# Seven half-size products for most tile pairs of both feed-forward stages, with the second matrix in five chunks

## Chip, cores and metric

The kernel runs on one core of a Trainium2 chip. The metric is the device time of one execution in microseconds (us); lower is better. All arithmetic is on fp32 data; the large products run on TensorE in its fp32r format, in three passes (below).

## What is computed

A trunk layer on h = 16 learned tokens followed by 512 tokens, 1024 features:

```python
h = h + 0.5 * rmsnorm(swiglu(rmsnorm(h, n[0]), ffn1_wi, ffn1_wo), n[1])
h = h + rmsnorm(hybrid_mixer(rmsnorm(h, n[2]), ...), n[3])
h = h + 0.5 * rmsnorm(swiglu(rmsnorm(h, n[4]), ffn2_wi, ffn2_wo), n[5])

def swiglu(x, wi, wo):                    # wi: 1024 x 5632, wo: 2816 x 1024
    a, b = jnp.split(x @ wi, 2, axis=-1)
    return (jax.nn.silu(a) * b) @ wo
```

The change touches the two feed-forward stages (`swiglu`). The mixer between them (Fourier, short convolution, gated DeltaNet) stays as it is.

## The kernel before

Features lie on the 128 partitions, tokens along the free dimension: `hT` is [128, 8, 528], eight feature tiles of all 528 tokens. The first feed-forward stage works on 528 tokens as two halves of 264 (one PSUM bank each); the second on the 512 real tokens, joined in one bank as one product of 512 columns, and in halves of 256 only next to the norms.

Every weight tile is one output tile of 128 features: `load` (lines 212 to 220) fetches 128x1024 floats with one DMA on SP's queue, ScalarE casts them to a high part `wh` (L219) and VectorE subtracts that for a low part `wl` (L220). `mm` (line 227) multiplies in three passes, (wh,xh), (wh,xl), (wl,xh), for each of the 8 feature tiles and each half; every matmul has a weight load of its own.

`ffn` (line 518) first forms 22 pairs (a, b): `wi[m]` and `wi[22+m]`, one `unit` each (24 matmuls per half). `scaled` (L504) multiplies by the norm's factor `rx` out of PSUM, L530 applies silu, `pair` (L526, L224, L225) multiplies a by b and splits the result into `gh`, `gl`, which hold all 22 tiles. Then each of the 8 output tiles of the second matrix is accumulated in PSUM over all 22 tiles (weights come in three pieces of 8, 8 and 6 tiles), and `evict_y` (line 305) copies it out and sums squares. The eighth tile is left to `tail`, which the following `edge` (line 375) or `finish` (line 431) runs half by half, so that the norm of the first half proceeds beside the products of the second. In `edge` each feature tile goes through `step`: L386 and L388 form the new h, L390 and L391 split h times gain into the next stage's input `x`; three units of the next stage follow these steps tile by tile. The next norm's factor `rx` comes later (L288, L275, L276).

The order of TensorE's instructions is written out by hand: it executes them in the order of the program. The other engines and the DMA queues are ordered when the program is built, by a list of priorities in program order; `high_priority(n)` moves instructions n places ahead. Each engine runs its own list strictly in order. A tile pool hands a buffer to the next tile that asks as soon as one is released by its last reader: `ws` has 2 buffers, `wh` and `wl` 3 each, the PSUM pools `pb` and `pd` 4 banks each.

Of the kernel before, what the change touches and what calls it, by code (L numbers as in the profile page):

```python
# [16 lines left out]
P = 128  # L17
NM = 16
S = 512
# [10 lines left out]
AHEAD = 150  # L30
XW = 5.0
# [23 lines left out]
# columns of the packed constants  # L55
# [45 lines left out]
class Cols:  # L101
    """Token columns of a stage, in two halves; joined: both fit one PSUM bank."""
# [17 lines left out]
class Tensor:  # L120
    """The tensor engine's instructions, with a sum of their length that orders the side work."""
# [22 lines left out]
class K:  # L144
    def __init__(self, tc, A, ctx):
        self.tc, self.nc, self.A = tc, tc.nc, A
        self.n = 0
        self.sides = []
        self.T = Tensor(tc.nc)
        e = ctx.enter_context  # L150
        self.cp = e(tc.tile_pool(name="cp", bufs=1))
        self.xp = e(tc.tile_pool(name="xp", bufs=1))
# [35 lines left out]
    # side work goes between the large products; it yields how far on its next part goes  # L188
# [22 lines left out]
    # weights: staged as stored, then split into two parts of 12 significand bits  # L211
    def load(self, src, nk=KD):
        nc = self.nc
        with self.tc.high_priority(AHEAD):
            st = self.t(self.wp, "ws", [P, KD, P], F32, 2)
            h = self.t(self.wp, "wh", [P, KD, P], F32R)
            l = self.t(self.wp, "wl", [P, KD, P], F32R)
# [9 lines left out]
    def mm(self, views, w, x, wk, xk, start, stop):  # L227
        """views += w[:, wk].T @ x[:, xk] by three exact passes"""
# [76 lines left out]
    def evict_y(self, ya, m, ps, gain=None, table=KD - 2):  # L305
        """ps: (half, what the products of tile m gave for it)"""
        y, acc = ya
        ACT, V = self.nc.scalar, self.nc.vector
        for i, p in ps:
            w = acc[i].shape[1]  # L310
            if gain is None:
                ACT.copy(y[i][:, m, :w], p)
            else:
                ACT.activation(y[i][:, m, :w], p, AF.Copy, scale=self.gains[:, gain, m:m + 1])
            if m == 0:
                ACT.activation(acc[i], p, AF.Square)
            else:
                sq = self.t(self.tp, "sy", [P, HN], F32, 1)[:, :w]
                ACT.activation(sq, p, AF.Square)  # L319
                V.tensor_tensor(acc[i], acc[i], sq, op=ALU.add)  # L320
        if m == table:
# [12 lines left out]
    def start(self, xT, gpre, srcs):  # L334
        """the first norm and tiles: everything arrives in the order of need"""
# [28 lines left out]
        # warm-up products while the first loads arrive  # L364
# [10 lines left out]
    def edge(self, C, hT, ya, gpost, gpre, tail, switch, nxt):  # L375
# [7 lines left out]
        def step(i, k):  # L383
# [4 lines left out]
            V.tensor_tensor(hT[:, k, c], hT[:, k, c], t, op=ALU.add)  # L388
            g = self.gains[:, gpre, k:k + 1]
# [4 lines left out]
        tiles, tx, tc = tail()  # L394
        for t in tiles:
            self.evict_y(ya, t[0], [(0, self.part(t, tx, tc[0], W))], table=tiles[0][0] - 1)
# [12 lines left out]
        for t in tiles:  # L409
            self.evict_y(ya, t[0], [(1, self.part(t, tx, tc[1], W, lambda: next(e, None)))], table=-1)  # L410
# [20 lines left out]
    def finish(self, hT, ya, tail, out):  # L431
        """the last norm and residual; the second half of the tokens goes by tokens"""
# [5 lines left out]
        (tile,), tx, tc = tail()  # L438
        last = tile[0]
# [8 lines left out]
        self.evict_y(ya, last, [(0, self.part(tile, tx, tc[0], W))], 5, -1)  # L448
# [36 lines left out]
        p = self.part(tile, tx, tc[1], W, lambda: next(e, None))  # L485
# [3 lines left out]
        ACT.activation(sq[:, :W], p, AF.Square)  # L489
        ACT.activation(y[1][:, last, :W], p, AF.Copy, scale=self.gains[:, 5, last:last + 1])  # L490
# [20 lines left out]
    def open_ffn(self):  # L511
        ctx = ExitStack()
        gp = ctx.enter_context(self.tc.tile_pool(name=self.uid("gp"), bufs=1))
        self.gp = gp
        self.t3 = lambda: self.t(gp, "t3", [P, 530], F32, 3)
        return ctx

    def ffn(self, pre, wi, wo, C, gain=None):
        nc = self.nc
        x, os = pre  # L520
        gh = self.t(self.gp, "gh", [P, KF, L], F32R)
        gl = self.t(self.gp, "gl", [P, KF, L], F32R)
        u = C.u

        def pair(m, a, b):
            nc.vector.tensor_tensor(a[:, u], a[:, u], b[:, u], op=ALU.mult)  # L526
            self.split(gh[:, m, u], gl[:, m, u], a[:, u])

        def silu(a):
            nc.scalar.activation(a[:, u], a[:, u], AF.Silu)  # L530

        y = self.ytile().rearrange("p k c -> p (k c)")
        a, b, a1 = (y[:, i * L:(i + 1) * L] for i in range(3))
# [4 lines left out]
        for t in (a, b):  # L538
            nc.vector.tensor_tensor(t[:, u], t[:, u], self.rx[:, u], op=ALU.mult)
        silu(a)  # L540
        pair(0, a, b)
        nc.vector.tensor_tensor(a1[:, u], a1[:, u], self.rx[:, u], op=ALU.mult)
        silu(a1)
        b = self.t3()
        self.scaled(b, o)
        pair(1, a1, b)
        for m in range(2, KF):
            a = self.t3()
            self.scaled(a, o2 if m == 2 else self.unit(wi[m], x, C))
            silu(a)  # L550
            b = self.t3()
            self.scaled(b, o3 if m == 2 else self.unit(wi[KF + m], x, C))
            pair(m, a, b)
        ya = self.start_y(C)
        chunks = [(k0, min(8, KF - k0)) for k0 in range(0, KF, 8)]
        g = (gh, gl)
        for m in range(KD - 1):
            o = self.outs(C)
            for k0, n in chunks:
                w = self.load(wo[m][:, k0:k0 + n], n)  # L560
                for k in range(n):
                    self.mm(o.full, w, g, k, k0 + k, k0 + k == 0, k0 + k == KF - 1)
            self.evict_y(ya, m, [(i, p) for i, (p, _) in enumerate(o.half)], gain)

        def tail():
            ws = [(self.load(wo[KD - 1][:, k0:k0 + n], n), n, k0) for k0, n in chunks]
            return [(KD - 1, [(w, k, k0 + k) for w, n, k0 in ws for k in range(n)])], g, C.halves
        return ya, tail

# [18 lines left out]
    def mixer(self, pre, hT):  # L588
# [100 lines left out]
        def tail():  # L689
            ws = [(m, self.load(A["wout"][m])) for m in range(KD - NT, KD)]  # L690
            return [(m, [(w, k, k) for k in range(KD)]) for m, w in ws], (mh, ml), CS.halves
# [39 lines left out]
    def fold(self, q, o, fh, fl):  # L731
# [13 lines left out]
        def fold():  # L745
# [18 lines left out]
            # token L - k for k = 1 .. L/2 - 1  # L764
# [30 lines left out]
    # per-token scalars of both directions, [token, head, direction, tile]; tile 4: meta tokens  # L795
# [6 lines left out]
    def ab(self, ab):  # L802
# [23 lines left out]
        # softplus(a) = max(a, 0) + 2 atanh(e / (2 + e)), e = exp(-|a|)  # L826
# [5 lines left out]
        # beta = 1 / (1 + exp(-x))  # L832
# [50 lines left out]
    # short conv and silu of one head's q, k or v  # L883
# [8 lines left out]
    # token-major copies and l2norm  # L892
# [38 lines left out]
    # both heads' k: l2norm, token-major and back  # L931
# [41 lines left out]
    def rsqrt(self, dst, src, scale=1.0):  # L973
        """1 / sqrt(src * scale + eps) of a few columns: a first value from the exponent, then Newton's steps"""
# [11 lines left out]
    # chunk matrices and the scan of a pair of heads, both directions  # L986
    def dn_core(self, st, slack):
# [6 lines left out]
        # [token, head * 2 + direction, tile]  # L994
# [11 lines left out]
        # exponents gc_i - gc_j, masked  # L1006
# [319 lines left out]
```

## Time and profile before

| | |
|---|---|
| median of 3 runs | 1327.61 us (1326.97 to 1329.06) |
| span of the profiled execution | 1325.0 us |
| TensorE busy | 1311.5 us (99%), 8575 matmuls |
| VectorE busy | 741.3 us (56%) |
| ScalarE busy | 492.3 us (37%) |
| mean granted TensorE clock | 0.999 |

The profile gives no separate total for the profiled execution. Its span runs from the first to the last instruction; the median of the timed runs is 2.6 us above it. The first feed-forward stage fills the span to about 394 us, the mixer from there to about 943 us, and the second feed-forward stage and the last norm the rest. Busy times count an instruction from its start to its modelled end, so that consecutive instructions of one engine overlap: the spacing of the starts tells what one more instruction costs.

### The profile page before, as it was taken

To read this page: it belongs to the slowest core of one execution; us is meant where nothing else is said; L and a number is where in the kernel's file an instruction comes from. 1 tells how busy PE (TensorE), PEld (TensorE's weight loads), DVE (VectorE), ACT (ScalarE), POOL (GpSimd) and SP (SyncE) were. 2 spreads that over 40 slices of the span, in tenths; PEclk is the share of its full clock that TensorE was granted. 3 is DMA by queue.
4 is the path that set the end of the run, shared out by engine and by line. 5 is a ranking of instruction groups with operands and counts; after the bars stand their busy time and mean duration, and the time that the engine had idled before them with its cause. 6 is when DMAs were issued, how large, how long until landed. Compare 5 with 4: busy or idle time off the path is not lost.

```text
span 1325.0 us, 20942 instructions
## 1 busy us (share of the span) xinstructions
PE 1311.5 (99%) x8575; PEld 1159.8 (88%) x8575; DVE 741.3 (56%) x1524; ACT 492.3 (37%) x911; POOL 4.7 (0%) x12
## 2 busy tenths in 40 slices
PE   9999999999999999999999999999999999999998
PEld 9999999999999988778987777888978888888887
DVE  6644444422239888758788578564774444442223
ACT  7322222222235452344633434334552222222222
POOL 0000000000000000000000000000000000000000
PEclk9999999999999999999999999999999999999999
DMA  6322323333225222322221222235133332333332
GB/s 196 96 83 93 95 81 96 91 84 94 88 85 189 85 72 89 107 70 70 75 65 60 70 64 66 87 102 175 49 112 95 95 96 96 95 92 95 96 90 74
DMA packets 49844, 123.05 MB, mean 93 GB/s; under 512 B 13388, under 2 KB 17612, under 8 KB 49748
## 3 DMA queue, kind: packets, MB, share of 16 engines
q1 hardware_dynamic: 44660, 120.14, 29.2%
q10 hardware_dynamic: 5088, 1.57, 0.5%
q8 instruction: 67, 1.10, 0.3%
q14 instruction: 29, 0.24, 0.1%
HBM read 116.42 MB, written 5.28 MB: 92 GB/s over the span
## 4 chain that ended last, share of the span: by engine, by line
PE 95%; DVE 2%; ACT 1%; DMA 0%; SPq 0%; issue 0%; DVEq 0%; ACTq 0%
PE pb L137 86%; PE pd L137 8%; PE pd L141 1%; DVE s L386 1%; DVE x L391 1%; DVE wl L220 0%; DVE h L388 0%; ACT wh L219 0%; DMA h<-in_xT 0%; ACT O L1170 0%; DVE acc L288 0%; DVE x L499 0%; PE pb L141 0%; SPq L352 0%; ACT vp L1179 0%
## 5 line engine op out<-in xcount | busy, mean ns | idle before, releaser
L137 PE MATMUL pb<-x,wh 128*128 128x264 f32 (+3 forms) x3296 | 720.5, 325 | 3.5 <-DVE x L391 1.4
L137 PEld LDWEIGHTS pb<-x,wh 128*128 128x128 f32 x3296 | 513.8, 188 | 59.8 <-issue 4.6
L137 PE MATMUL pb<-x,wl 128*128 128x264 f32 (+3 forms) x1648 | 450.2, 323 | 1.1 <-DVE wl L220 1.0
L219 ACT CAST wh<-ws 128x1024 fp32r<-128x1024 f32 (+2 forms) x222 | 219.2, 988 | 613.3 <-PE pb L137 589.0
L220 DVE TENSOR_TENSOR wl<-ws,wh 128x1024 fp32r<-128x1024 f32 (+2 forms) x222 | 253.8, 1144 | 197.4 <-ACT wh L219 196.8
L137 PEld LDWEIGHTS pb<-x,wl 128*128 128x128 f32 x1648 | 276.5, 188 | 26.8 <-DVE wl L220 1.9
L504 DVE TENSOR_TENSOR t<-pb,rx 128x264 f32<-128x264 f32 (+2 forms) x144 | 67.7, 499 | 228.8 <-PE pb L137 228.8
L137 PE MATMUL pb<-gh,wh 128*128 128x264 f32 (+2 forms) x550 | 149.0, 316 | 0.0
L137 PE MATMUL pb<-gh,wl 128*128 128x264 f32 (+2 forms) x550 | 148.0, 315 | 0.0
L137 PE MATMUL pb<-gl,wh 128*128 128x264 f32 (+2 forms) x550 | 147.6, 314 | 0.0
L137 PEld LDWEIGHTS pb<-gl,wh 128*128 128x128 f32 x550 | 93.2, 188 | 6.9
L137 PEld LDWEIGHTS pb<-gh,wh 128*128 128x128 f32 x550 | 93.2, 188 | 6.5
L137 PEld LDWEIGHTS pb<-gh,wl 128*128 128x128 f32 x550 | 93.1, 188 | 6.6
L137 PE MATMUL pb<-y,wh 128*128 128x512 f32 x192 | 61.7, 402 | 0.0
L137 PEld LDWEIGHTS pb<-y,wh 128*128 128x128 f32 x192 | 34.4, 188 | 8.5 <-issue 2.2
L137 PE MATMUL pb<-y,wl 128*128 128x512 f32 x96 | 37.5, 391 | 0.0
L224 ACT CAST gh<-t 128x528 fp32r<-128x528 f32 (+1 forms) x40 | 25.1, 628 | 31.1 <-DVE t L526 31.1
L700 DVE TENSOR_TENSOR t<-pb,rx 128x512 f32<-128x512 f32 x24 | 16.6, 690 | 32.0 <-PE pb L137 32.0
L137 PE MATMUL pd<-x,wh 128*128 128x264 f32 (+2 forms) x176 | 33.3, 294 | 0.0
L1179 ACT ACTIVATE vp<-pd,be 64x128 f32<-64x128 f32 x64 | 23.2, 363 | 21.1 <-PE pd L137 19.8
L320 DVE TENSOR_TENSOR acc<-acc,sy 128x256 f32<-128x256 f32 (+1 forms) x41 | 17.4, 424 | 24.0 <-ACT sy L319 24.0
L526 DVE TENSOR_TENSOR t<-t,t 128x528 f32<-128x528 f32 (+1 forms) x40 | 28.0, 699 | 3.8
(261 smaller groups left out, 1113.1 us busy)
## 6 DMA issues: line engine op xcount, KB each, us to landing
ws<-in_wi SPq DMA_DIRECT2D x85, 512.0 KB, 3.5
ws<-in_wo SPq DMA_DIRECT2D x32, 512.0 KB, 3.4
ws<-in_win SPq DMA_DIRECT2D x32, 512.0 KB, 3.5
ws<-in_wg SPq DMA_DIRECT2D x24, 512.0 KB, 3.4
ws<-in_wo SPq DMA_DIRECT2D x16, 384.0 KB, 3.2
ws<-in_wout SPq DMA_DIRECT2D x8, 512.0 KB, 3.4
keep<-h SPq DMA_DIRECT2D x1, 2048.0 KB, 7.9
ws<-in_wsc SPq DMA_DIRECT2D x8, 256.0 KB, 2.7
```

The source lines that it names most:

```text
L137: return self.e.matmul(out, lhsT, rhs, **kw)
L141: return self.e.transpose(*a)
L219: nc.scalar.copy(h[:, :nk], st[:, :nk])
L220: nc.vector.tensor_tensor(l[:, :nk], st[:, :nk], h[:, :nk].bitcast(F32), op=ALU.subtract)
L224: self.nc.scalar.copy(h, src)
L320: V.tensor_tensor(acc[i], acc[i], sq, op=ALU.add)
L386: V.scalar_tensor_tensor(t, ya[0][i][:, k, :W], self.gains[:, gpost, k:k + 1], r[:, c], op0=ALU.mult, op1=ALU.mult)
L391: V.scalar_tensor_tensor(x[1][:, k, c], hT[:, k, c], g, x[0][:, k, c].bitcast(F32), op0=ALU.mult, op1=ALU.subtract)
L504: self.nc.vector.tensor_tensor(dst[:, c.start + off:c.stop + off], p, self.rx[:, c], op=ALU.mult)
L526: nc.vector.tensor_tensor(a[:, u], a[:, u], b[:, u], op=ALU.mult)
L700: nc.vector.tensor_tensor(g, o.full[0][0], self.rx[:, NM:], op=ALU.mult)
L1179: ACT.activation(v1[X, hd], b[X, hd * P:(hd + 1) * P], AF.Copy, scale=beta[X, hd, t:t + 1])
```

## The change

Tile pairs 0 to 3 are formed as before. Each of the pairs 4 to 21 is computed by a seven-product scheme for 2x2 block matrices (Strassen's in Winograd's form): the activation's blocks are the two token halves times the two halves of the features, the weight's blocks are the two halves of the features of `wi[m]` and `wi[22+m]`. A product is 4 feature tiles in three passes over one token half: 12 matmuls of 264 (second stage: 256) columns. Each pair takes 84 such matmuls; before it took 96 of 264, or 48 of 512.

`seven` forms the eight activation blocks once per stage, from h times gain times `rx`, in place in `hT`; `hT` is fetched again later from memory (first stage: the input; second: a copy `keep` that `edge` writes with DMAs on ScalarE's queue). `pair_load` fetches a pair's weights in four DMAs of 128x512, forms four sums on VectorE and splits seven blocks. Partial sums of the products stay in PSUM (`bank0`, two of `bank1`, `bank2`), with copies on ScalarE and additions on VectorE between them.

The 22 tiles of the hidden layer are cut into five chunks of 4, 4, 4, 5, 5. The second matrix is multiplied chunk by chunk: 8 output tiles times 4 or 5 feature tiles ("second tiles"). Chunk 0 is copied into y, the others are added to y on VectorE. Second tiles of the chunk before are set between the products of a pair (`slot`). The last chunk runs at the end, its last three tiles in `tail`.

```diff
+AHEAD2 = 200
+URGENT = 450
+CHUNKS = (range(0, 4), range(4, 8), range(8, 12), range(12, 17), range(17, 22))
+NU = max(len(c) for c in CHUNKS)
+FIRST = 5
...
     def load(self, src, nk=KD, second=False):
...
+            if second:
+                h, l = (self.t(self.gp, n, [P, NU, P], F32R, 2) for n in ("uh", "ul"))
...
     def evict_y(self, ya, m, ps, gain=None, table=KD - 2, more=False):
...
+            if more:
+                V.tensor_tensor(y[i][:, m, :w], y[i][:, m, :w], p, op=ALU.add)
+                p = y[i][:, m, :w]
...
     def edge(self, C, hT, ya, gpost, gpre, tail, switch, nxt, keep=None):
...
+            if keep is not None:
+                nc.scalar.dma_start(keep[:, k, i * W:(i + 1) * W], hT[:, k, c])
...
     def finish(self, hT, ya, tail, out):
...
-        ACT.activation(sq[:, :W], p, AF.Square)
-        ACT.activation(y[1][:, last, :W], p, AF.Copy, scale=self.gains[:, 5, last:last + 1])
+        z = y[1][:, last, :W]
+        V.tensor_tensor(z, z, p, op=ALU.add)
+        ACT.activation(sq[:, :W], z, AF.Square)
+        ACT.activation(z, z, AF.Copy, scale=self.gains[:, 5, last:last + 1])
...
+    def seven(self, hT, C, gpre):
...
+        for k in range(KD):
+            V.scalar_tensor_tensor(hT[:, k, C.u], hT[:, k, C.u], self.gains[:, gpre, k:k + 1], self.rx[:, C.u],
+                                   op0=ALU.mult, op1=ALU.mult)
...
+        put(1, h3[:, 0, :, :W], l3[:, 0, :, :W], A11)
+        V.tensor_tensor(s, A21, A22, op=ALU.subtract)
+        put(5, h3[:, 1, :, :W], l3[:, 1, :, :W], s)
+        put(2, h3[:, 2, :, :W], l3[:, 2, :, :W], A12)
+        V.scalar_tensor_tensor(s, s, -1.0, A11, op0=ALU.mult, op1=ALU.subtract)
+        V.tensor_tensor(A21, A11, A21, op=ALU.add)
+        V.scalar_tensor_tensor(A12, A12, -1.0, s, op0=ALU.mult, op1=ALU.subtract)
...
+    def pair_load(self, w1, w2):
...
+        with self.tc.high_priority(AHEAD2):
+            fa, fb, fc, fd = (self.t(self.gp, "wf", [P, KD, P], F32, 4) for _ in range(4))
+            lo, hi = slice(0, 4), slice(4, 8)
+            nc.sync.dma_start(fa[:, lo], w1[:, lo])
+            nc.sync.dma_start(fd[:, hi], w2[:, lo])
+            nc.sync.dma_start(fb[:, lo], w1[:, hi])
+            nc.sync.dma_start(fc[:, hi], w2[:, hi])
...
+            V.tensor_tensor(fa[:, hi], fa[:, lo], fd[:, hi], op=ALU.add)
+            put(fa, 1, 5)
+            V.tensor_tensor(fb[:, hi], fa[:, hi], fc[:, hi], op=ALU.add)
+            put(fb, 2, 6)
+            V.tensor_tensor(fc[:, lo], fd[:, hi], fc[:, hi], op=ALU.add)
+            put(fc, 7, 3)
+            V.tensor_tensor(fd[:, lo], fb[:, hi], fb[:, lo], op=ALU.add)
+            put(fd, 4, None, 4, "w4", self.gp, 1)
...
+        between(get(0, 0), get(0, 1))
+        for m in range(2, FIRST):
+            whole(0, m)
+        later = [(0, m) for m in range(FIRST, KD)]
...
+        def slot(rate):
+            nonlocal acc
+            acc += rate
+            if acc >= 0.999 and later:
+                acc -= 1.0
+                whole(*later.pop(0))
...
+        for ci in range(1, len(CHUNKS)):
+            n = len(CHUNKS[ci])
+            for m in CHUNKS[ci]:
+                if m == CHUNKS[ci].start + 1:
+                    while later:
+                        whole(*later.pop(0))
+                    acc = 0.0
+                    if ci > 1:
+                        later = [(ci - 1, i) for i in range(KD)]
+                    else:
+                        later = [(0, i) for i in range(FIRST, KD)]
+                rate = (KD if ci > 1 else KD - FIRST) / (2.0 * n)
+                nxt = one(m)
+                five(nxt)
+                slot(rate)
+                if st:
+                    seven(st)
+                slot(rate)
+                two(nxt)
+                if st:
+                    four(st)
+                six(nxt)
+                st = nxt
...
+        while later:
+            whole(*later.pop(0))
+        four(st)
+        fin = len(CHUNKS) - 1
+        between(get(fin, 0, False), get(fin, 1, False))
+        for m in range(2, KD - 3):
+            whole(fin, m, False)
```

`one` to `seven` run the products of that number (`seven` also runs product 3) and what follows each on ScalarE or VectorE; `whole` loads and multiplies one second tile and evicts it; `between` does so for two tiles, keeping the last feature tile of both back.

## Rows read from the trace of the kernel before

**Rows 1.** The page's first part: span, busy time of each engine, share, instructions.

```profile
span 1325.0 us, 20942 instructions
PE 1311.5 (99%) x8575; PEld 1159.8 (88%) x8575; DVE 741.3 (56%) x1524; ACT 492.3 (37%) x911; POOL 4.7 (0%) x12
```

**Rows 2.** Windows: us; busy PE, PEld, DVE, ACT, POOL (instructions); clock; DMA; GB/s.

```profile
100.00:140.00 40.00, 40.00 (x329) 40.00 (x328) 18.93 (x29) 11.54 (x14) 0.00 (x0) 1.00 0.28 86
...
390.00:420.00 30.00, 28.04 (x220) 26.71 (x220) 28.70 (x71) 19.89 (x46) 0.20 (x2) 1.00 0.47 165
...
480.00:520.00 40.00, 39.32 (x294) 36.28 (x293) 34.69 (x88) 13.70 (x29) 1.19 (x2) 1.00 0.29 87
```

**Rows 3.** Timeline of PE: first and last of 66, of 61 and of 66 matmuls.

```profile
377.90 0.28 PE L137 MATMUL pb<-gh,wh 128*128 128x264 f32 x1
...
385.79 0.28 PE L137 MATMUL pb<-gh,wl 128*128 128x264 f32 x1
...
1283.77 0.39 PE L137 MATMUL pb<-gh,wl 128*128 128x512 f32 x1
...
1297.62 0.40 PE L137 MATMUL pb<-gh,wl 128*128 128x512 f32 x1
1297.86 0.28 PE L137 MATMUL pb<-gh,wh 128*128 128x256 f32 x1
...
1305.50 0.28 PE L137 MATMUL pb<-gh,wl 128*128 128x256 f32 x1
```

**Rows 4.** Groups by line and shape: busy us, mean ns | idle before, releasers.

```profile
L220 DVE TENSOR_TENSOR wl<-ws,wh 128x1024 fp32r<-128x1024 f32 x182 | 222.1, 1221 | 156.5 <-ACT wh L219 155.9
L219 ACT CAST wh<-ws 128x1024 fp32r<-128x1024 f32 x182 | 191.0, 1050 | 505.6 <-PE pb L137 489.8 <-issue 10.9 <-DMA ws<-in_wout 1.8
...
L504 DVE TENSOR_TENSOR t<-pb,rx 128x264 f32<-128x264 f32 x98 | 37.9, 426 | 120.4 <-PE pb L137 120.4
...
L220 DVE TENSOR_TENSOR wl<-ws,wh 128x512 fp32r<-128x512 f32 x24 | 16.4, 682 | 1.5 <-ACT wh L219 1.4
...
L219 ACT CAST wh<-ws 128x512 fp32r<-128x512 f32 x24 | 14.9, 620 | 54.5 <-PE pb L137 46.0 <-issue 6.5 <-ACT EZ L1124 1.9
...
L526 DVE TENSOR_TENSOR t<-t,t 128x512 f32<-128x512 f32 x20 | 13.8, 691 | 1.9
...
L386 DVE SCALAR_TENSOR_TENSOR s<-y,gains,r 128x264 f32<-128x264 f32 x16 | 7.4, 485 | 0.1
...
L361 DVE SCALAR_TENSOR_TENSOR x<-h,gains,x 128x528 fp32r<-128x528 f32 x8 | 6.1, 763 | 2.4 <-ACT x L360 2.4
```

**Rows 5.** DMA issues: KB each, median us from issue to landing.

```profile
ws<-in_wsc SPq DMA_DIRECT2D x8, 256.0 KB, 2.7
```

**Rows 6.** Timeline of DVE, last split of tile pair 2, in each feed-forward stage.

```profile
47.10 0.71 DVE L225 TENSOR_TENSOR gl<-t,gh 128x528 fp32r<-128x528 f32 x1 [0.70 <-ACT gh L224]
...
983.77 0.69 DVE L225 TENSOR_TENSOR gl<-t,gh 128x512 fp32r<-128x512 f32 x1 [0.69 <-ACT gh L224]
```

**Rows 7.** Chain of waits, in order of time: the two feed-forward stages, the last norm.

```profile
42.77 345.15 PE pb L137 x2829
...
979.99 327.57 PE pb L137 x1455
...
1317.82 0.71 PE pb L137 x6
```

**Rows 8.** Timeline of DVE and ScalarE's queue in the last norm.

```profile
1315.01 0.75 DVE L462 TENSOR_TENSOR h<-h,s 128x256 f32<-128x256 f32 x2
...
1311.44 0.40 ACTq L463 DMA_DIRECT2D out<-h  x1
```

**Rows 9.** The page's fifth part, weight loads of the second matrix: busy us, mean ns.

```profile
L137 PEld LDWEIGHTS pb<-gh,wh 128*128 128x128 f32 x550 | 93.2, 188 | 6.5
```

More of the change, by code (lines that the diff above doesn't have):

```diff
@@ L437, in finish @@
         y, acc = ya
-        (tile,), tx, tc = tail()
-        last = tile[0]
+        tiles, tx, tc, more = tail()
+        last = tiles[-1][0]
         outA = out[:, :KD * W].rearrange("p (k c) -> p k c", k=KD)
@@ L447, in finish @@
         yT = []
-        self.evict_y(ya, last, [(0, self.part(tile, tx, tc[0], W))], 5, -1)
+        for t in tiles:
+            self.evict_y(ya, t[0], [(0, self.part(t, tx, tc[0], W))], 5, -1, more)
         bs = []
@@ L484, in finish @@
         e = early()
-        p = self.part(tile, tx, tc[1], W, lambda: next(e, None))
+        for t in tiles[:-1]:
+            self.evict_y(ya, t[0], [(1, self.part(t, tx, tc[1], W, lambda: next(e, None)))], 5, -1, more)
+        p = self.part(tiles[-1], tx, tc[1], W, lambda: next(e, None))
         for _ in e:
@@ L547, in ffn @@
[L547 to L553, printed above, removed]
+        self.scaled(b1, o)
+        pair(1, a1[:, u], b1[:, u])
+        e = self.ev()
+        self.scaled(e[:, 0], o2)
+        silu(e[:, 0])
+        self.scaled(e[:, 1], o3)
+        pair(2, e[:, 0, u], e[:, 1, u])
+        e = self.ev()
@@ L554, in ffn, with second @@
+        o, o2 = self.unit(wi[3], x, C), self.unit(wi[KF + 3], x, C)
+        with urgent():
+            self.scaled(e[:, 0], o)
+            silu(e[:, 0])
+            self.scaled(e[:, 1], o2)
+            pair(3, e[:, 0, u], e[:, 1, u])
+        X, rest = self.seven(hT, C, gpre)
+        rest()
         ya = self.start_y(C)
-        chunks = [(k0, min(8, KF - k0)) for k0 in range(0, KF, 8)]
-        g = (gh, gl)
-        for m in range(KD - 1):
+        later = []
+        def second(ci, m, w):
+            n = len(CHUNKS[ci])
+            final = ci == len(CHUNKS) - 1
@@ L558, in ffn, with ks, evict @@
             o = self.outs(C)
[L559 to L563, printed above, removed]
+            def ks(r):
+                for k in r:
+                    self.mm(o.full, w, G[ci], k, k, k == 0, k == n - 1)
+            def evict():
+                ps = [(i, p) for i, (p, _) in enumerate(o.half)]
+                with urgent():
+                    if final:
+                        return self.evict_y(ya, m, ps, gain, more=True)
+                    for i, p in ps:
+                        y = ya[0][i][:, m, :W]
+                        if ci:
+                            V.tensor_tensor(y, y, p, op=ALU.add)
+                        else:
+                            ACT.copy(y, p)
@@ new lines, in ffn, with one, five @@
+        class Pair:
+            pass
+        def one(m):
+            st = Pair()
+            st.m, st.w = m, self.pair_load(wi[m], wi[KF + m])
+            if m == CHUNKS[1].start:
+                for b in (*bank1, bank2):
+                    T.matmul(b, st.w[1][0][:, 0], X[1][0][:, 0], start=True, stop=True)
+            st.b1 = bank1[m % 2]
+            product(1, st, bank0, True)
+            with urgent():
+                ACT.copy(st.b1, bank0)
+            return st
+        def five(st):
+            b4 = self.big()[:, :W]
+            product(5, st, b4, True)
+            st.p5 = self.t(self.gp, "p5", [P, HN], F32, 2)[:, :W]
+            with urgent():
+                ACT.copy(st.p5, b4)
```

162 lines of the change are left out of this document (128 added, 34 removed).

## The prediction

> **What bounds the kernel now.** I read the page's first part, then windows over the feed-forward stages, then the chain of waits. TensorE is busy 99% of the span; VectorE 56%, ScalarE 37% [rows 1]. In a feed-forward window TensorE has no idle time and VectorE works less than half of it (first of [rows 2]). In the chain, 345.15 us of the first stage and 327.57 us of the second are TensorE pieces with no wait between them [rows 7]. So both stages are bound by the number and width of the matmuls, and VectorE and ScalarE have time to give. TensorE is short of work only at the norms: 390 to 420 us has 1.96 us of idle time, with VectorE at 28.70 of 30 us (second of [rows 2]).
>
> **Price of a matmul.** From the spacing of starts [rows 3]: 264 columns (385.79 - 377.90)/65 = 0.1214 us; 512 columns (1297.62 - 1283.77)/60 = 0.2308; 256 columns (1305.50 - 1297.86)/65 = 0.1175. Two products of 256 thus cost 0.2350, 2% more than one of 512.
>
> **First matrix.** 18 pairs a stage. First stage: 18x96 = 1728 matmuls become 18x84 = 1512, and 3 that open the banks: 213 fewer, -25.9 us. Second stage: 18x48 = 864 of 512 columns (199.4 us) become 1515 of 256 (178.0 us): -21.4.
>
> **Second matrix.** The diff builds the list of chunk 0's tiles 5 to 7 before the loop. During pair 4 the slots count 0.375 and 0.75 and run none; at pair 5 the list is emptied, all three tiles run, and then the same list is built again. These three tiles are multiplied twice (they are copied, not added, so nothing else changes): 3x4x3x2 = 72 matmuls of 264, +8.7 us. Second stage: 36 of 512 more; besides, the tail runs 3 tiles of 5 instead of one of 22 in halves, so 42 products of 256 go and 21 of 512 come. Together 57x0.2308 - 42x0.1175 = +8.2.
>
> TensorE's sum: -25.9 - 21.4 + 8.7 + 8.2 = **-30.4 us**.
>
> **VectorE's load.** Per pair [rows 4]: four sums of 128x512 at 0.691, three splits at 1.221 and one at 0.682, two evictions of one bank (0.426, 0.485), product and split of the hidden tile (2x0.69): 9.4 us; before, the same pair took 2.44 + 4x0.426 + 1.4 = 5.5. A second tile adds 0.682 for its weights and 2x0.426 to add it to y: 1.5. With two second tiles between the products an iteration takes TensorE 84x0.1214 + 48x0.1214 = 16.0 us and VectorE 12.5 (78%); with one, 13.1 and 10.9 (83%). The mixer's window from 480 to 520 us has VectorE at 87% and TensorE idle for only 0.68 of 40 us (third of [rows 2]), so such a load needn't bind. ScalarE casts 3x1.05 + 0.62 = 3.8 us of weights a pair instead of 2.1 and has more room. I take nothing for it, and VectorE's cover is what remains, 2 to 3 us an iteration.
>
> **The longest new chain.** `pair_load` has one set of four staging buffers, handed on in order of release. Last to be released is `fd`: its block 4 can be split only when product 4 of the pair before has been read by TensorE (the `w4` tiles have one buffer). The fourth DMA of the next pair (`fc`) takes that buffer. SP's queue is strict: weights of second tiles issued behind it wait with it. From the end of product 4: cast 0.62, split 0.68, DMA of 256 KB 2.7, sum 0.69, cast 1.05, split 1.22 [rows 4, 5] = 7.0 us until product 2 of the next pair can start. TensorE meanwhile has products 6, 1, 5, 7 and 3, 60 matmuls: 7.3 us (second stage 7.05), and one second tile (2.9; 2.8) in 7 iterations of a stage, two in the others, by counting the slots. So the margin is 3 us in 14 iterations and 6 us in the rest. Against it stand waits in the queues: three turns on VectorE, each behind at most a 1.22 us split, two on ScalarE behind at most a 1.05 us cast: 0 to 5.8 us, none in a VectorE that idles. Stall: 0 to 2.8 us in 14 iterations, 0 to **39 us** in all. Nearer to the lower end, since an engine 80% busy holds an arrival for a fraction of one instruction: 0.2 each, **+2.8**.
>
> **Start of the products.** `seven` puts about 15 us on VectorE before product 2 and 5 more before the second pair: eight scalings (0.763), four sums and splits of 1056 columns (about 1.25 each, estimated from the 1.221 of 1024). VectorE is free of the first three pairs at 47.8 us and 984.5 us [rows 6]. By product 6 of pair 4 it owes 28 us: a unit's split 1.2, pair 3 3.1, `seven` 16.7, five second tiles' weights 3.4, `pair_load` up to `fb` 3.8. TensorE gets there after two units, five second tiles and three products: 42.77 + 11.7 + 14.6 + 4.4 = 73.4 us, so 25.6 us of time. In the second stage: 979.99 + 11.1 + 13.8 + 4.2 = 1009.1, 24.6 us against 27. Deficit 2.4 in each by mean durations; but two VectorE instructions in a row take 0.75, not 2x0.42 [rows 8], which takes some 7% off. Between 0 and 2.4 each: 1 each, **+2.0**. The three tiles at pair 5 then let VectorE catch up.
>
> **The norms.** In `edge` after the first stage, the products of the second half cover the first half's norm. 66 matmuls become 45, so 21x0.1214 = 2.6 us of cover go, and the addition to y lies on the chain (0.43). VectorE was at its limit there already: **+3.0**, between 0.4 and 3.0. `finish`: the same 21 matmuls (2.5) go from beside VectorE's last additions, which ended at 1315.8, 1.9 before the products' end [rows 7, 8]; four more VectorE instructions for the tiles 5 and 6 (1.5) and the addition before the last square (0.43) lie before the end: **+3.0**, between 0.5 and 3.5. The 16 DMAs of `keep` on ScalarE's queue: one entry there took 0.40 [rows 8], so 0 to 6.4; VectorE sets the pace of `step`, so **+0.5**. The DMAs that bring h back are 16 of some 264 KB on SP, no one needs them before the edge: 0; if that cover failed, one landing, 2.7 us.
>
> **Sum** against the profiled execution: 1325.0 - 30.4 + 2.8 + 2.0 + 3.0 + 3.0 + 0.5 = 1305.9 us of span. The median of the runs lies 2.6 above that span: **1308.5 us**, 1.4% faster.
>
> A rule that speaks against the change: the Trainium skill, page "TensorE: Matmul & The Clock Gate", section Part 3, says that a weight load overlaps a running matmul only when its row group differs. Every load here is 128x128, so none would overlap. By that rule the second stage, whose number of loads rises, would lose. The rows disagree: a load is recorded with each matmul [rows 1], at 188 ns [rows 9], and matmuls of 256 columns start every 117.5 ns [rows 3].
>
> **Rivals.**
> - *No stall at all.* For it: the margins above, and VectorE's 87% window. Against it: the cover at both norms is taken away whatever the queues do. 1325.0 - 30.4 + 2.6 + about 2.8 for the norms = 1300 us. Chance 0.12.
> - *The staging chain decides* (the other side). If waits in the queues lengthen the 7.0 us chain by 5 us everywhere, one-tile iterations lose 2 us and whatever SP's queue holds up behind `fc` makes second tiles late too. Each us by which the 34 iterations are late on average costs 34 us; it decides from 0.6 us an iteration, when the 21.9 us that are left after the starts and norms are used up. At 1 us: 1303 + 2.6 + 34 = 1340 us. For it: a static order in which casts, splits and evictions of three pairs share two queues. Against it: two second tiles in most iterations. Chance 0.13.
> - *VectorE binds part of the way*: the starts at 2.4 each and 1 us in the 14 tight iterations: 2.8 more at the starts and 14: 1303 + 2.6 + 2.8 + 14 = 1322 us. For it: 83% and a chain that returns to VectorE three times. Against it: the window at 87%. Chance 0.08.
> - *The loop does less than I read*, the three tiles once: 17 us off, 1292 us. The diff's text is against it. Chance 0.01.
> - *Weight loads stand alone*: the second stage has 1515 + 519 + 90 - 864 - 462 - 132 = 666 more of them, at 0.188 us: +125, 1434 us. This is the rule of the Trainium skill's page "TensorE: Matmul & The Clock Gate" above. The rows are against it. Chance 0.01.
>
> **How the numbers follow.** The forecast (1303 to 1318, queue waits small) has 0.65. A difference within 0.2% (2.7 us) of 1327.6 is about what a measurement of this kernel can't tell from none. Faster: 0.65 + 0.12 + 0.01 + half of the third rival 0.04 = 0.82. Same: the other half of it, 0.04. Slower: 0.13 + 0.01 = 0.14. The range reaches from just below the case without stalls, 1299, to some us above the third rival, 1328; outside lie the two slower cases and the single count of tiles, some 0.15, and the forecast's own error.
>
> **What would show it.** TensorE's instructions rise from 8575 to about 8575 - 141 + 666 = 9100, most of 264 and 256 columns; three second tiles of chunk 0 appear twice. VectorE's busy time rises to about 980 us (per stage 18x3.9 for pairs, 20 for `seven`, 28 for additions to y). Between the products TensorE's idle time should be under 10 us in both stages together; idle pieces of over 1 us ahead of product 2, ended by a VectorE split or by `fc`'s DMA, would make the second rival right. Idle time in the first edge should grow from 1.96 to about 5 us, and VectorE's last additions should end after the products in `finish`. If matmuls of 256 columns start further apart than 0.12 us in the mixed stage, or if stalls recur in each iteration, the prediction is wrong.

## The result, and the profile after

The changed kernel takes **1310.51 us** (median of 4 runs, 1309.77 to 1310.99) against 1327.39 us of the kernel before beside it: ratio 0.9872, 95% interval 0.9858 to 0.9886. The prediction was 1308.5 us. The difference is 1.3%, where 1.4% was predicted. The profiled execution's span is 1309.0 us, 16.0 less than before; its sum had 1305.9.

Page of the changed kernel, part 1 and one line of part 6 (the counterparts of [rows 1] and [rows 5]):

```profile
span 1309.0 us, 23064 instructions
...
PE 1286.5 (98%) x9100; PEld 1166.7 (89%) x9100; DVE 958.1 (73%) x1908; ACT 622.4 (48%) x1205; POOL 4.7 (0%) x12
...
wf<-in_wi SPq DMA_DIRECT2D x144, 256.0 KB, 2.6
```

9100 matmuls, exactly the count foreseen, so the three tiles of chunk 0 are multiplied twice; a pair's DMA lands in 2.6 us, about as priced. Windows of the changed kernel (columns as in [rows 2]): a stretch of products, two of the first edge (the norms after the first feed-forward stage), one of the second edge (the norms ahead of the second feed-forward stage) and what follows it.

```profile
100.00:140.00 40.00, 40.00 (x332) 40.00 (x332) 29.39 (x41) 22.20 (x41) 0.00 (x0) 1.00 0.32 105
360.00:400.00 40.00, 36.14 (x288) 34.66 (x288) 33.80 (x82) 22.26 (x48) 0.20 (x2) 1.00 0.35 112
400.00:420.00 20.00, 19.20 (x153) 18.64 (x153) 16.84 (x31) 10.51 (x19) 0.00 (x0) 1.00 0.61 214
940.00:960.00 20.00, 15.19 (x95) 13.03 (x94) 18.52 (x35) 12.22 (x25) 0.00 (x0) 0.98 0.44 145
960.00:980.00 20.00, 20.00 (x76) 16.00 (x77) 18.08 (x25) 10.56 (x14) 0.00 (x0) 0.85 0.18 54
```

Among the products TensorE doesn't wait, with VectorE at 73%: the timeline has no idle piece of 0.2 us or more from 61 to 370 us, nor from 985 to 1300. The time not foreseen is in the fourth and fifth row: 4.81 us idle, then 76 matmuls in 20 us and a granted clock of 0.85. The waits behind it, from the timeline of TensorE (start, duration, instruction, idle time before and what ended it); the first two are the first edge's, the last is the last norm's:

```profile
374.46 0.63 PE L142 MATMUL pd<-ones,acc 128*88 128x1 f32 x6 [1.11 <-DVE acc L332]
382.76 0.39 PE L142 MATMUL pb<-x,wh 128*128 128x264 f32 x1 [1.09 <-DVE x L407]
959.76 1.19 PE L142 MATMUL pd<-acc,ones 128*128 128x256 f32 x2 [3.95 <-DVE acc L297]
1301.31 0.58 PE L142 MATMUL pb<-ones,acc 128*128 128x1 f32 x4 [1.25 <-DVE acc L332]
```

The third is new: the second of the two matmuls that form `rx` for the second feed-forward stage waits 3.95 us for the norm's sums (`xstat`, L297). In the kernel before, the two (four records) ran one behind the other, without a wait:

```profile
968.55 1.02 PE L137 MATMUL pd<-acc,ones 128*128 128x256 f32 x4
```

Timeline of VectorE in the changed kernel, ahead of the wait:

```profile
944.80 0.42 DVE L297 TENSOR_TENSOR acc<-acc,sx 128x256 f32<-128x256 f32 x1
945.14 0.69 DVE L602 TENSOR_TENSOR wf<-wf,wf 128x512 f32<-128x512 f32 x1
...
946.47 0.69 DVE L604 TENSOR_TENSOR wf<-wf,wf 128x512 f32<-128x512 f32 x1
947.07 0.42 DVE L297 TENSOR_TENSOR acc<-acc,sx 128x256 f32<-128x256 f32 x1
947.41 0.69 DVE L606 TENSOR_TENSOR wf<-wf 128x512 f32<-128x512 f32 x1
948.03 2.36 DVE L229 TENSOR_TENSOR wl<-ws,wh 128x1024 fp32r<-128x1024 f32 x2
...
951.26 0.69 DVE L234 TENSOR_TENSOR w4l<-wf,w4h 128x512 fp32r<-128x512 f32 x1
...
957.25 0.42 DVE L297 TENSOR_TENSOR acc<-acc,sx 128x256 f32<-128x256 f32 x1
957.59 1.75 DVE L285 RECIPROCAL rx<-rx 128x256 f32<-128x256 f32 x1
959.25 0.36 DVE L297 TENSOR_TENSOR acc<-acc,sx 128x256 f32<-128x256 f32 x1
```

The sums and one split of the first seven-product pair (L602, L604, L606, `w4l`: 2.8 us) stand between the norm's sums, some 50 us before that pair's products, which start at 999: `pair_load` is moved 200 places ahead. The last sum also stands behind the reciprocal of the first half (1.75 us). And the wait has a second price. Windows of the changed kernel around it:

```profile
957.00:959.00 2.00, 0.00 (x0) 0.00 (x0) 2.00 (x3) 0.06 (x1) 0.00 (x0) 1.00 0.53 136
959.00:961.00 2.00, 1.24 (x3) 1.09 (x4) 0.95 (x3) 0.63 (x2) 0.00 (x0) 0.50 0.21 81
961.00:963.00 2.00, 2.00 (x6) 1.52 (x6) 1.85 (x2) 0.46 (x1) 0.00 (x0) 0.50 0.31 62
963.00:966.00 3.00, 3.00 (x9) 2.33 (x8) 2.93 (x6) 2.01 (x3) 0.00 (x0) 0.53 0.15 54
966.00:970.00 4.00, 4.00 (x19) 3.24 (x18) 3.47 (x5) 3.13 (x5) 0.00 (x0) 1.00 0.23 66
```

After the idle time TensorE is granted 0.50, 1.2 instead of 2.4 GHz, for some 7 us: 3 matmuls a microsecond instead of nearly 5.

### The profile page after: what moved, and what is told of

The parts are those of the page before. It is cut to its first block, busy times and chain, and to the rows that moved or that the text cites. A ratio compares the mean times of both kernels' runs of the same rounds, so it can differ in the third digit from the quotient of the medians.

```text
span 1309.0 us, 23064 instructions
## 1 busy us (share of the span) xinstructions
PE 1286.5 (98%) x9100; PEld 1166.7 (89%) x9100; DVE 958.1 (73%) x1908; ACT 622.4 (48%) x1205; POOL 4.7 (0%) x12
## 3 DMA queue, kind: packets, MB, share of 16 engines
q10 hardware_dynamic: 7392, 3.67, 0.9%
## 5 line engine op out<-in xcount | busy, mean ns | idle before, releaser
L142 PE MATMUL pb<-x,wh 128*128 128x264 f32 (+3 forms) x1568 | 355.8, 331 | 4.6 <-DVE x L407 2.5
L142 PEld LDWEIGHTS pb<-x,wh 128*128 128x128 f32 x1568 | 247.4, 190 | 36.2 <-issue 4.6
L142 PE MATMUL pb<-x,wl 128*128 128x264 f32 (+3 forms) x784 | 220.4, 326 | 1.1 <-DVE wl L229 1.0
L142 PE MATMUL pd<-x,wh 128*128 128x264 f32 (+2 forms) x1040 | 191.9, 284 | 0.0
L142 PEld LDWEIGHTS pd<-x,wh 128*128 128x128 f32 x1040 | 160.2, 188 | 1.8
L234 DVE TENSOR_TENSOR wl<-wf,wh 128x1024 fp32r<-128x1024 f32 x108 | 130.0, 1223 | 28.3 <-ACT wh L233 27.9
L142 PEld LDWEIGHTS pb<-x,wl 128*128 128x128 f32 x784 | 133.9, 190 | 14.6 <-DVE wl L229 1.7
L229 DVE TENSOR_TENSOR wl<-ws,wh 128x1024 fp32r<-128x1024 f32 (+2 forms) x114 | 121.2, 1066 | 34.8 <-ACT wh L228 34.3
L142 PE MATMUL pd<-x,wl 128*128 128x264 f32 (+2 forms) x520 | 143.9, 284 | 0.0
L142 PE MATMUL pb<-gh,uh 128*128 128x264 f32 (+2 forms) x484 | 130.2, 319 | 0.4 <-ACT gh L233 0.4
```

Of the source, the lines that this page charges most:

```text
L142: return self.e.matmul(out, lhsT, rhs, **kw)
L229: nc.vector.tensor_tensor(l[:, :nk], st[:, :nk], h[:, :nk].bitcast(F32), op=ALU.subtract)
L234: self.nc.vector.tensor_tensor(l, src, h.bitcast(F32), op=ALU.subtract)
```

## Experiments

All are set against the changed kernel's 1310.51 us; each ratio is to the kernel before. To compare single profiles, one mark serves: the start of the second `pd<-ident,rt` of the norm ahead of the second stage, 934.35 in the changed kernel, 374.65 us before the end of its span. In profiles of different kernels a wait for the very first weights, near 11 us, alone moves all later starts by up to 1 us. Where the products are compared, the stretch runs from the first matmul of chunk 0's second tiles to the matmul that takes the norm's last sums (374.46 and 1301.31 in the rows above): 320.0 us in the first stage and 316.7 in the second.

**The doubled tiles once, in the slots.**

```diff
-        later = [(0, m) for m in range(FIRST, KD)]
+        later = []
```

> The list that is built before the loop is left empty, so chunk 0's tiles 5 to 7 are multiplied once, in the slots of pairs 5 to 7; the other copy of them, 36 products of 264 and 36 of 512 columns a time, goes. Theory (both stages are bound by TensorE's sum of matmuls, nothing else sets a time between the products): the time falls by 72 x 0.1214 = 8.7 us and 36 x 0.2308 = 8.3 us, 17.0 in all, to about 1293.5 us, with windows of the product stretches still full. Rival (the doubled tiles are the cover behind which VectorE catches up after the eight activation blocks are formed): TensorE waits near pair 5, the gain is 10 us or less, 1300 or more.

1295.91 us, ratio 0.9758 (0.9744 to 0.9773): 14.6 us less by medians, 15.3 by spans. The products start with waits of 0.31 and 0.42 us and have none after. The theory holds: the doubled tiles were no cover that VectorE needed. The two stretches of products are 8.2 and 8.0 us shorter, 16.2 of the 17.0. The products begin 0.8 us later. The clock falls once more than in the changed kernel, to 0.50 for 3.4 us in the first edge, but behind the wait for `rx` it also stays there for only 3.4 us instead of 7, and the two about cancel.

**The doubled tiles once, all at pair 5.**

```diff
-                    else:
-                        later = [(0, i) for i in range(FIRST, KD)]
```

> The second build of the list is dropped instead, so the three tiles are multiplied once, all at pair 5, and pairs 5 to 8 have no second tile between their products: an iteration of TensorE is 84 x 0.1214 = 10.2 us there. Theory (the spare time of VectorE, 9.4 us of work a pair, and of the staging chain, 7.0 us against 7.3 of cover, suffices): the same 17.0 us, about 1293.5 us, no waits among the products. Rival (without a second tile the staging chain or VectorE sets the iteration): waits of 1 to 3 us in each of the three bare iterations of a stage, 6 to 12 us of the gain lost, 1299 to 1306 us, and slower than the other single count by that.

1305.65 us, 0.9843 (0.9826 to 0.9859): in the rival's range, and waits in all three bare iterations of each stage. Timeline of TensorE, ScalarE, VectorE and SP's queue at two of the waits:

```profile
116.31 0.28 PE L142 MATMUL pd<-x,w4l 128*128 128x264 f32 x1
116.67 1.23 DVE L234 TENSOR_TENSOR wl<-wf,wh 128x1024 fp32r<-128x1024 f32 x1 [1.16 <-ACT wh L233]
116.83 0.61 ACT L233 CAST w4h<-wf 128x512 fp32r<-128x512 f32 x1
117.82 0.68 DVE L234 TENSOR_TENSOR w4l<-wf,w4h 128x512 fp32r<-128x512 f32 x1
...
118.53 0.33 SPq L591 DMA_DIRECT2D wf<-in_wi  x1
...
121.26 0.69 DVE L602 TENSOR_TENSOR wf<-wf,wf 128x512 f32<-128x512 f32 x1 [0.73 <-DMA wf<-in_wi]
...
121.98 2.00 ACT L233 CAST wh<-wf 128x1024 fp32r<-128x1024 f32 x2 [0.61 <-DVE wf L602]
...
123.07 1.22 DVE L234 TENSOR_TENSOR wl<-wf,wh 128x1024 fp32r<-128x1024 f32 x1
...
124.32 0.33 SPq L589 DMA_DIRECT2D wf<-in_wi  x1
124.35 0.39 PE L142 MATMUL pd<-h,wl 128*128 128x264 f32 x1 [0.24 <-DVE wl L234]
...
127.04 0.69 DVE L600 TENSOR_TENSOR wf<-wf,wf 128x512 f32<-128x512 f32 x1 [0.93 <-DMA wf<-in_wi]
...
128.01 1.04 ACT L233 CAST wh<-wf 128x1024 fp32r<-128x1024 f32 x1
...
129.08 1.23 DVE L234 TENSOR_TENSOR wl<-wf,wh 128x1024 fp32r<-128x1024 f32 x1
...
130.36 0.39 PE L142 MATMUL pd<-h,wl 128*128 128x264 f32 x1 [0.75 <-DVE wl L234]
```

As far as 124.35 that is the prediction's staging chain, link by link: last matmul of product 4, cast, split, DMA into the buffer it frees (2.73 us), sum, cast, split, product 2 of the next pair: 124.35 - 116.43 = 7.9 us, 0.9 of it in queues (the cast starts 0.4 late, the `w4l` split stands 0.4 behind a 1.23 us split). But the chain doesn't end there. The split that product 2 waits for frees one more buffer, whose DMA starts at 124.32, and DMA, sum, cast and split follow once more until product 1 of the pair after it can go on: 130.36 - 124.35 = 6.0 us, for which products 2, 4 and 6 leave 36 x 0.1214 = 4.4. Most of the waiting is at this second end: of 6.1 us in six iterations, 4.5 are ahead of a product 1 and 1.6 ahead of a product 2.

**That chain cut at either of two links**, on top of the kernel just shown: two buffers for product 4's weights, or five staging buffers.

```diff
-            put(fd, 4, None, 4, "w4", self.gp, 1)
+            put(fd, 4, None, 4, "w4", self.gp, 2)
```

```diff
-            fa, fb, fc, fd = (self.t(self.gp, "wf", [P, KD, P], F32, 4) for _ in range(4))
+            fa, fb, fc, fd = (self.t(self.gp, "wf", [P, KD, P], F32, 5) for _ in range(4))
```

> On top of the variant that drops the second build of the list (1305.65 us, with 6.1 us of waits in pairs without a second tile), the tiles of product 4's weights get two buffers instead of one, so that their split needn't wait until product 4 of the pair before is through. Theory (those waits are the chain product 4, split, release of the staging buffer, fourth DMA, sum, cast, split: 7.9 us in that trace against 7.3 of cover): the waits go, about 1299.5 us. Rival (VectorE's 9.4 us of work a pair, in 10.2 us, makes them, whatever the buffers): no change within 2 us of 1305.7.

> On top of the same variant, five staging buffers for the pairs' weights instead of four: the fourth DMA of the next pair no longer waits for the one that product 4's split releases. Theory (the same chain, cut at another link): the waits go, about 1299.5 us. Rival (VectorE's work): no change within 2 us of 1305.7.

1296.25 us, 0.9760 (0.9744 to 0.9777), and 1294.60 us, 0.9755 (0.9739 to 0.9772): the theory in both, and 3 to 5 us below its 1299.5. Windows with four staging buffers, then with five:

```profile
100.00:140.00 40.00, 37.54 (x301) 36.49 (x300) 31.93 (x46) 20.29 (x34) 0.00 (x0) 1.00 0.31 101
1020.00:1060.00 40.00, 36.30 (x282) 34.33 (x281) 30.98 (x44) 20.29 (x34) 0.00 (x0) 1.00 0.29 94
```

```profile
100.00:140.00 40.00, 40.00 (x332) 40.00 (x331) 33.13 (x50) 20.08 (x34) 0.00 (x0) 1.00 0.31 94
1020.00:1060.00 40.00, 39.97 (x314) 38.72 (x313) 32.55 (x50) 21.07 (x36) 0.00 (x0) 1.00 0.32 98
```

The waits are gone while VectorE works more of the time (33.13 of 40 us, 83%), so it was the chain and not VectorE's load. The counts also tell more than the idle time: 31 and 32 matmuls more in 40 us are 31 x 0.1214 + 32 x 40/314 = 7.8 us, where the idle time is 2.46 + 3.67 = 6.1, since a matmul's modelled end lies beyond the start of the next. Over the two whole stretches of products it is 4.6 + 5.6 = 10.2 us, about the 9.8 between the two spans.

**More work per pair.**

```diff
-            V.tensor_tensor(fa[:, hi], fa[:, lo], fd[:, hi], op=ALU.add)
+            for _ in range(3):
+                V.tensor_tensor(fa[:, hi], fa[:, lo], fd[:, hi], op=ALU.add)
```

> Each pair's first sum of 128x512 is done three times instead of once, with the same result: 2 x 0.69 = 1.4 us more on VectorE and ScalarE idle for as long, ahead of every cast of a pair. From the pairs without any second tile, which lost 1.15 to 1.35 us each, the staging chain is some 1.2 us longer than 84 products; one second tile covers 2.9, so 1.7 us an iteration should be left. Theory (the spare in one-tile iterations is 1.7 us): the products stay without waits, and only the norms, where VectorE is full, lose up to 1.4 us each: 1310 to 1313. Rival (the spare is smaller than 1.4 us, the prediction's second rival just behind the edge): waits of some 0.5 us or more in 14 iterations, 1317 or more.

1319.62 us, 0.9942 (0.9919 to 0.9965). The rival's time, though its waits don't show in 14 iterations: four have waits of 1.2 to 1.5 us, one in the first stage and three in the second, and two others less than 0.4; 5.6 us in all. One of them, in TensorE's timeline:

```profile
1056.68 0.39 PE L142 MATMUL pd<-h,wh 128*128 128x256 f32 x1 [0.71 <-ACT wh L233]
1057.94 0.39 PE L142 MATMUL pd<-h,wl 128*128 128x256 f32 x1 [0.76 <-DVE wl L234]
```

Idle time counts too little here as well: the two stretches of products are 3.7 and 9.6 us longer than the changed kernel's. In the second, 1.6 of these go to waits for `gh` ahead of the pairs (1.35 of them at 993.88) and 1.7 to a clock of 0.50 for 3.4 us after them. So the changed kernel has, in these iterations, less than 1.4 us to spare, where 10.2 - 7.9 = 2.3 us were to be expected from the chain to product 2. The trace shows where the rest went: all of these waits but one of 0.19 us stand ahead of product 1, behind the very sum that is now done three times. As far as product 1 the chain takes 130.36 - 116.43 = 13.93 us in the trace above, and with one second tile on the way TensorE has 96 x 0.1214 + 2.9 = 14.55 us of other work: an estimate of 0.6 us to spare. Whether VectorE's longer queue adds to it is not separated by this run.

**The wait for rx: the sums moved ahead, far and a little.**

```diff
+                with self.tc.high_priority(URGENT):
                     sq = self.t(self.tp, "sx", [P, HN], F32, 2)[:, :W]
                     ACT.activation(sq, hT[:, k, c], AF.Square)
                     V.tensor_tensor(acc, acc, sq, op=ALU.add)
```

> The squares and their sums for the norm's factor are given priority over the weights of the first seven-product pair; nothing is added or left out. Theory (the 3.95 us wait ahead of the second rx matmul of the second stage comes from the pair's four sums and splits standing ahead of these sums in VectorE's order, and the half clock after it comes with the wait): the wait shrinks to under 0.5 us, the granted clock stays at 1.00 between 959 and 966, and 6.9 us go: about 1303.6 us. Rival (VectorE is simply full in that stretch and the wait moves to the next thing that is late): less than 2 us, over 1308.5.

1315.03 us, 0.9906 (0.9891 to 0.9921): slower by 4.5. The 3.95 us wait is gone, and the steps of the norm wait in its place. Timeline of TensorE in the second edge:

```profile
935.27 0.39 PE L142 MATMUL pb<-x,wh 128*128 128x256 f32 x1 [1.13 <-DVE x L408]
...
941.56 0.79 PE L142 MATMUL pd<-ident,rt 128*128 128x128 f32 x4 [1.43 <-DVE rt L285]
957.54 0.73 PE L142 MATMUL pb<-x,wh 128*128 128x512 f32 x2 [1.36 <-ACT wh L228]
```

The first edge has such waits too, and a clock of 0.50 from 389 to 396; in the second edge the clock is at 0.50 from 942 to 945 and from 959 to 962. With `high_priority(40)` in place of `URGENT`:

> The squares and sums of the norm's factor are moved ahead by 40 places, not 450: on VectorE they then stand behind nearly all steps of the norm and ahead of the first units' weight splits and of the first seven-product pair's sums. Theory (the order around these sums makes the wait): the 3.95 us wait falls to under 1 us without waits ahead of it, and up to 6.9 us go, about 1304 us. Rival (VectorE has more work in these 20 us than time, whichever goes first): the weight splits of the first units come up to 8 x 0.43 = 3.4 us later, TensorE waits for them near 949 instead, and the time stays within 2 us of 1310.5.

1309.65 us, 0.9861 (0.9845 to 0.9876), within 2 us, as the rival had it. From the mark to the end it takes 371.6 us, 3.0 less than the changed kernel, as the clock stays at 1.00 there; ahead of the mark it lost nearly as much, 2.6 us (0.9 us for the first weights; in the first edge 3.4 us at a clock of 0.50, and waits of 0.75 and 0.35 us for steps that the sums now precede). The wait itself has moved: 0.75 us for a unit's weights and 1.25 for `gl`.

**The wait for rx: covered.** First with dummy products that keep TensorE busy:

```diff
+                if C.joined and dst is parts[1][1]:
+                    for _ in range(16):
+                        self.T.e.matmul(ps[:, :P], self.ones, self.ones, start=True, stop=True)
                 self.T.matmul(ps, self.ones, acc, start=True, stop=True)
```

> Sixteen products of ones by ones, 128 columns each, are put ahead of the second rx matmul of the second stage, into a bank that this matmul then overwrites; the output doesn't change. They fill the wait and shorten nothing else. Theory (the clock falls because TensorE stood idle for 3.95 us): the wait for the sums is covered, the granted clock stays at 1.00 between 959 and 966, the 12 to 20 matmuls after it go at 0.231 us instead of 0.456, and about 3 us go: 1307.5 us. Rival (the clock falls there for another reason, such as what the other engines do): the clock still falls to 0.50 and the time stays within 1 us of 1310.5.

1308.61 us, 0.9856 (0.9842 to 0.9871); from the mark to the end 371.7 us, 3.0 less. Windows of this kernel over the same stretch:

```profile
958.00:962.00 4.00, 3.69 (x20) 3.00 (x19) 2.80 (x4) 2.28 (x3) 0.00 (x0) 1.00 0.21 61
962.00:966.00 4.00, 4.00 (x19) 3.24 (x18) 3.97 (x7) 2.20 (x3) 0.00 (x0) 1.00 0.20 61
```

The clock stays at 1.00 with nothing changed but TensorE's idle time: here it is the idleness that makes it fall, and the fall costs 3.0 us. (1 us of the 3.0 is missing in the medians' 1.9, with a fall to 0.50 in this profile's first edge.)

And the matmuls of `rx` later, behind 10 instead of 5 us of other work:

```diff
-XW = 5.0
+XW = 10.0
```

> The matmuls of the norm's factor rx are set later in TensorE's order, from 5.0 to 10.0 us of other work after the norm's sums; nothing is added or left out. Theory (the 3.95 us wait is only a matter of TensorE coming to the second rx matmul before VectorE has the last sum, at 959.3): with some 5 us more of products ahead of it, TensorE doesn't wait and its clock doesn't fall, 6.9 us go, about 1303.6 us. Rival (what needs rx, the scaling of the first pairs and the eight activation blocks, is then late by as much, and TensorE waits there): less than 2 us, or more waits between 975 and 1010.

1309.67 us, 0.9858 (0.9840 to 0.9876). Behind the mark 371.2 us, 3.5 less: no fall of the clock, and of the wait itself only some of it, as it moves to what needs `rx`. Timeline of TensorE:

```profile
983.74 0.51 PE L142 MATMUL pb<-gl,uh 128*128 128x512 f32 x1 [1.74 <-DVE gl L234]
...
1002.91 0.39 PE L142 MATMUL pd<-x,wh 128*128 128x256 f32 x1 [0.55 <-DVE x L234]
```

Ahead of the mark the later `rx` of the first stage costs 1.72 us at 45.78. So both theories are right in part: the clock's 3 us come back, VectorE's lateness doesn't.

**A longer tail**, four tiles instead of three:

```diff
-        for m in range(2, KD - 3):
+        for m in range(2, KD - 4):
...
-            ws = [(m, self.load(wo[m][:, c.start:c.stop], len(c), m < KD - 1)) for m in range(KD - 3, KD)]
+            ws = [(m, self.load(wo[m][:, c.start:c.stop], len(c), m < KD - 2)) for m in range(KD - 4, KD)]
```

> The tail that each norm is set beside gets four second tiles instead of three; nothing is added or left out in total, but 15 products of 264 (in the last norm 256) columns, 1.8 us, are moved from ahead of the first half's norm to beside it, and one more addition to y with them. Theory (the edge's 2.7 us and part of the finish's 1.7 are lost cover): up to 1.8 us of the first edge's idle 4.66 goes and some 1 us in the last norm, about 1308 us. Rival (VectorE, not the number of products beside it, sets the pace of both norms): no change within 1 us, 1310.5.

1310.61 us, 0.9866 (0.9841 to 0.9891): no difference. From the mark to the end it has 373.7 us, 1.0 less, as the theory had it for the last norm. In the first edge the idle time falls, but the clock falls too, to 0.50 for 10.2 us. One window of that edge:

```profile
382.00:394.00 12.00, 10.89 (x51) 10.11 (x51) 10.03 (x29) 5.21 (x13) 0.00 (x0) 0.57 0.37 138
```

The changed kernel ran 80 matmuls in these 12 us. The runs of the kernel with the longer tail, from 1308.69 to 1313.2, leave the edge's part inconclusive.

**What was found, together.** The tiles once, in the slots, and the later `rx` in the second stage alone:

```diff
-        self.side(gen(), XW)
+        self.side(gen(), 10.0 if C.joined else XW)
...
-        later = [(0, m) for m in range(FIRST, KD)]
+        later = []
```

> Chunk 0's tiles 5 to 7 once, in the slots, and in the second stage alone the matmuls of rx set later (10.0 instead of 5.0). Theory (the two gains add): the single count's 14.6 us, and of the rx wait the 3.0 us of half clock and some 0.5 us of the wait itself: 1310.5 - 14.6 - 3.5 = 1292.4 us. Rival (once the doubled tiles no longer cover VectorE, the later rx delays the activation blocks and the gain of 3.5 is lost): 1296.

1292.98 us, 0.9740 (0.9726 to 0.9755): 1.3% less than the changed kernel. Its page:

```profile
span 1290.4 us, 22799 instructions
...
PE 1267.1 (98%) x8992; PEld 1148.9 (89%) x8992; DVE 951.2 (74%) x1902; ACT 614.8 (48%) x1187; POOL 4.7 (0%) x12
```

The 108 matmuls fewer are the doubled tiles (72 + 36). With two buffers for product 4's weights (the edit above) and a tail of four tiles in the last norm:

> The same as the kernel with the single count and the later rx, with two buffers for product 4's weights and a tail of four second tiles instead of three in the last norm alone. Theory (slots leave some iterations without a second tile, whose waits the buffer removes, under 1 us in that trace; a longer tail gave 1.0 us in the last norm): 1.0 to 2.0 us less, about 1291 us. Rival (neither part is on the path): 1292.4.

1293.61 us, 0.9744 (0.9729 to 0.9758): the rival's time. But its profile has the clock at 0.50 for 3.4 us at 368 and again at 975, which the other's doesn't have; 6.8 us at half the clock hold 3.4 us less work. So what the two parts are worth by themselves is not shown. The five staging buffers were not tried together with the later `rx`.

## Why the prediction was right, and where it was not

- **TensorE's sum, -30.4 us.** Right in count; the single-count kernels bear out its largest doubtful part, the doubled tiles at 17 us (14.3 to 15.9 measured by medians, in the three kernels where nothing else stalls; 16.2 over the products alone in the first of them). One term was mis-sized: matmuls of 256 columns among the products start every 0.1189 us, not every 0.1175, which 1512 of them make +2.1 us. The chain of waits of the changed kernel shows it (8.56/72):

```profile
1029.32 8.56 PE pd L142 x72
```

- **Weight loads.** The second stage has 666 more of them and these matmuls still start every 0.119 us, well under one load's 188 ns [rows 9]. The rule weighed in the prediction (the Trainium skill, page "TensorE: Matmul & The Clock Gate", section Part 3) doesn't hold for these loads. The same section of the Trainium skill also has a load into the background weight buffer pulled ahead of running matmuls, which the prediction left out; the rows show loads of 128x128 running beside matmuls, and no run here shows into which buffer.
- **The staging chain, +2.8.** 0 was measured, as nothing waits among the products. The chain itself is real: 7.0 us foreseen, 7.9 measured as far as product 2, and decisive as soon as the second tile beside it goes. What the prediction left out is its second end, product 1 of the pair after, and so it put the margin at 3 us in the iterations with one second tile, where an estimated 0.6 are left. The second rival named the right chain, not its cause: 0.9 us were spent in queues, not 5; the tiles between the products keep the chain from deciding.
- **VectorE's load.** 958 us, 980 foreseen; its 83% don't bind, as five staging buffers show.
- **Start of the products, +2.0.** 0.7: two short waits in the first stage (0.38 and 0.23) and next to none in the second. That the three tiles at pair 5 let VectorE catch up was not needed.
- **The first edge, +3.0.** By idle time alone: from 360 to 420 us it is 3.86 + 0.80 = 4.66 us, against the 1.96 of [rows 2]: +2.7.
- **Finish, +3.0.** 1.7: from the tail's first matmul to the end of the span, less 0.1175 us for each of its matmuls, it is 27.1 - 132 x 0.1175 = 11.6 us before and 23.9 - 90 x 0.1175 = 13.3 after. TensorE now waits for VectorE's last additions (the row at 1301.31), in the order foreseen. **Keep, +0.5:** the other waits of the second edge are 0.4 longer together; that `keep` makes them is not shown.
- **The step that failed** is the third part of the norms: the prediction priced the edge after the first stage and the last norm, and for the edge ahead of the second stage only the DMAs of `keep`. It counted what VectorE owes from the end of pair 2 (984.5) on, not what the first pair's early sums displace at 945. That wait and the half clock behind it cost 3.95 + 3.0 = 6.9 us. Moving the sums ahead, far or a little, only moved the wait, as VectorE is full there (busy for all of the 14 us from 936 to 950); covering the wait gives back the 3 us of clock. That these early sums make the wait is read from VectorE's order: a kernel in which that pair's weights come later was not run.

Together: -30.4 + 2.1 + 0.7 + 2.7 + 1.7 + 0.4 + 6.9 = -15.9 us, against -16.0 in the spans. So close an agreement is chance, as the terms from idle time count too little. That the sum of the prediction came within 3.1 us of the span is luck in part, too: the staging chain, the start, the edge, the finish and `keep` were priced 5.8 us too high together, and against that stand 2.1 + 6.9 = 9.0 us that it didn't have.

## What to carry to other kernels

A prefetch with high priority takes its place from whatever the engine does at that time: look at what stands in the order where it lands, not only at what waits for it. A chain through a handed-on buffer is priced from the last reader to the next user, link by link, and then on through the buffer that this user's weights free; one more buffer cut it here at either of two links. And when an idle TensorE can't be helped, the clock behind the wait is a cost of its own: other work set into the wait paid here although the wait only moved (2.9 us, between the two kernels with the tiles once, in the slots).

## What was not expected of the hardware

The clock's price: 3.95 us of idle time was followed by some 7 us at 0.50, 3.0 us in cost, and in all seven profiles that have this wait (3.60 to 4.39 us) the clock fell to 0.50 near its end, for 3.4 to 6.8 us. Of the six kernels in which it was covered or moved, four kept 1.00 in that place and two lost it after two shorter waits in a row (1.36 and 0.53 us; 1.10 and 1.79). In the first edge it is less regular still: idle pieces of up to 2.2 us follow each other within 15 us, and in 8 of 13 profiles with the seven products the clock then fell to 0.50 for 3.4 to 10.2 us; in 5, that of the changed kernel among them, it didn't fall there at all. At its worst (51 matmuls instead of 80 in 12 us) that is more than the edits tried there were worth.
